# A batched 64x64 matmul kernel: four of the eight a tiles are loaded two product tiles later

## The chip, the cores and the metric

The kernel runs on one core of a Trainium2 chip. The metric is the device time of one execution in microseconds (us), as the median of several runs. One more execution was recorded by the hardware profiler. All rows of "the profile" and "the trace" come from that one.

## The reference

```python
def setup_inputs():
    return {
        "a": np.random.randn(1024, 64, 64).astype(np.float32),
        "b": np.random.randn(1024, 64, 64).astype(np.float32),
    }

def reference(a, b):
    return np.matmul(a, b).astype(np.float32)
```

There are 1024 independent products of two 64x64 matrices. The inputs and the output are fp32 and take 16.8 MB each.

## The kernel before

**Tiles.** The work is cut into 16 *product tiles*, t = 0 to 15, of 64 products each. Product tile t needs one *b tile* of 1 MB, called b t below, and half of an *a tile*. There are eight a tiles, s = 0 to 7, of 2 MB each. a tile s serves the product tiles 2s and 2s + 1. Each product tile ends in a *store* of 1 MB, called store t.

**Loads.** An a tile comes in four parts (`load_a`). Three of them go through GpSimd's (POOL's) DMA queue and are turned into bf16 on the way (line 74). The fourth stays fp32 and goes through SyncE's (SP's) DMA queue (line 78). The first a tile is loaded in another way and plays no part here. b tiles (`load_b`, line 97) go through SP's queue for even t and through ScalarE's (ACT's) queue for odd t. Stores go through POOL's queue (line 195), and only the last two product tiles are stored through SP's and ACT's. So POOL's queue carries most of each a tile and most stores, one after the other, and SP's queue carries the fourth parts of the a tiles and half of the b tiles.

**Work on a product tile.** TensorE needs a transposed. For s = 2 to 5 VectorE (DVE) does it, with 32x32 block transposes (line 128, `transpose_dve`), one half of the a tile per product tile, after ACT has cast the fp32 part (line 126). For the other a tiles DVE first copies the tile into one bf16 tile (`regroup`, lines 109 and 112), TensorE transposes (line 138) and ACT copies the result out of PSUM (line 141). Then DVE copies the blocks of one product tile into a block-diagonal operand (`spread`, lines 154 and 164) and casts the b tile to bf16 (`cast`, line 173; the last one is shared with ACT, lines 178 and 180). TensorE multiplies (line 218), ACT copies the product to SBUF (line 206), and the store is issued one product tile later.

**Buffers.** There are three buffers for a tiles 1 to 7 and three for b tiles, eight for output tiles. a tile 4 goes where a tile 1 was, a tile 5 where a tile 2 was, and so on. Loading b tile t + 3 has to wait for the cast of b tile t.

**Order.** The order of the instructions is written out by hand (`tc.manual_schedule()`). Each engine executes its own instructions in that order, and a DMA is issued by the engine that owns its queue, in that engine's order. In the pass of the loop for product tile t the order is: spread and cast of tile t + 1, load of b tile t + 3, now and then a load of an a tile, the multiplication of tile t, preparation of the a tile that is two further on, and the store of tile t - 1. Before the loop, a tiles 0, 1 and 2 and b tiles 0, 1 and 2 are asked for. a tiles 3 and 4 are asked for in the pass t = 0, then a tiles 5, 6 and 7 in the passes t = 2, 4 and 6.

The preparation of a tile s on DVE starts in the pass t = 2s - 4 (from s = 3 on). So a tile 6 is regrouped in the pass t = 8, after the cast of b tile 9, and a tile 7 in the pass t = 10, after the cast of b tile 11. Both are on DVE, which runs in order: what comes later in its order (the spread and cast for tile 12 behind a tile 7) waits with it.

Of the kernel before, what the change touches and what calls it, by code (L numbers as in the profile page):

```python
# [13 lines left out]
def kernel(  # L14
# [19 lines left out]
    n_t, n_s = B // 64, B // 128  # L34
    A_AHEAD = 3
# [34 lines left out]
    def load_a(s):  # L70

        a_sb = a_pool.tile([128, 3, 16, 64], bf16, name="a_sb")
        for h in range(3):
            nc.gpsimd.dma_start(  # L74
                out=a_sb[:, h, :, :].rearrange("p v k -> p (v k)"), in_=a_v[s, h], single_packet=True
            )
        a_raw = a_pool.tile([128, 16, 64], fp32, name="a_raw")
        nc.sync.dma_start(out=a_raw[:].rearrange("p v k -> p (v k)"), in_=a_v[s, 3])
        a_tiles[s] = a_sb, a_raw

    def load_first_a():

        raw = [
            o_pool.tile([128, 8, 2, 2, 64], fp32, name="o_sb")[:].rearrange(
                "p gh j wl n -> p (gh j wl n)"
            )
            for _ in range(2)
        ]
        parts = [raw[h % 2][:, 1024 * (h // 2) : 1024 * (h // 2) + 1024] for h in range(4)]
        for h in range(4):  # L90
            (nc.scalar if h % 2 else nc.sync).dma_start(out=parts[h], in_=a_v[0, h])
        a_tiles[0] = parts

    def load_b(t):
        b_sb = b_pool.tile([128, 16, 128], fp32, name="b_sb")
        queue = nc.scalar if t % 2 else nc.sync
        queue.dma_start(out=b_sb[:], in_=b_v[t])  # L97
        b_tiles[t] = b_sb

    def regroup(s):  # L100
        a_sb = a_tiles.pop(s)
        a_bf = work.tile([128, 16, 4, 64], bf16, name="a_bf")
        if s == 0:
            for h in range(4):
                copy = nc.scalar.copy if h % 2 else nc.vector.tensor_copy
                copy(a_bf[:, :, h, :], a_sb[h].rearrange("p (v k) -> p v k", v=16))  # L106
        else:
            cast_sb, raw = a_sb
            nc.vector.tensor_copy(  # L109
                a_bf[:, :, 0:3, :], cast_sb[:].rearrange("p h v k -> p v h k")  # L110
            )
            nc.vector.tensor_copy(a_bf[:, :, 3, :], raw[:])  # L112
        abf_tiles[s] = a_bf
        at_tiles[s] = work.tile([128, 32, 4, 4, 4], fp32, name="at_sb")

    def transpose_dve(s, half):
        cast_sb, raw = a_tiles[s]
        if half == 0:
            at_tiles[s] = work.tile([128, 4, 8, 4, 4, 4], fp32, name="at_sb")
        for h in (2 * half, 2 * half + 1):  # L120
            rows = cast_sb[:, h, :, :] if h < 3 else None
            if h == 3:
                rows = work.tile([128, 16, 4, 64], bf16, name="a_bf")[:, 0:4, :, :].rearrange(
                    "p x y k -> p (x y) k"
                )
                nc.scalar.copy(rows, raw[:])  # L126
            pairs = rows.rearrange("p v k -> p (v k)").bitcast(fp32)
            nc.vector.transpose(  # L128
                at_tiles[s][:, h].rearrange("p g w mp vo -> p w vo g mp"),
                pairs.rearrange("p (vo w kp) -> p w vo kp", vo=4, w=4),  # L130
            )

    def transpose(s, j):
        a_cols = abf_tiles[s][:].rearrange("p v h k -> p v (h k)").bitcast(fp32)
        for wl in range(2):
            at_ps = t_psum.tile([128, 4, 128], fp32, name="at_ps")
            for vo in range(4):
                nc.tensor.transpose(  # L138
                    at_ps[:, vo, :], a_cols[:, 4 * vo + 2 * j + wl, :], identity[:]
                )  # L140
            nc.scalar.copy(  # L141
                at_tiles[s][:, :, 2 * j + wl, :, :],
                at_ps[:].rearrange("p vo (g mp) -> p g mp vo", mp=4),
            )

    def spread(t):
        bd = bd_tiles[t % N_BD]
        at_sb = at_tiles[t // 2]
        for h in range(4):
            rows = slice(32 * h, 32 * h + 32)  # L150
            if t // 2 in ON_DVE:
                for i in range(2):
                    block = 32 * (2 * (t % 2) + i)
                    nc.vector.tensor_copy(  # L154
                        bd[rows, 8 * i : 8 * i + 8, :, h, :, :].rearrange(
                            "p g w mp vo -> p (g w) (mp vo)"
                        ),
                        at_sb[block : block + 32, h].rearrange(
                            "p g w mp vo -> p (g w) (mp vo)"
                        ),  # L160
                    )
            else:
                half = slice(16 * (t % 2), 16 * (t % 2) + 16)
                nc.vector.tensor_copy(  # L164
                    bd[rows, :, :, h, :, :].rearrange("p g w mp vo -> p (g w) (mp vo)"),
                    at_sb[rows, half].rearrange("p g w mp vo -> p (g w) (mp vo)"),
                )

    def cast(t):
        b_bf = work.tile([128, 16, 128], bf16, name="b_bf")  # L170
        b_sb = b_tiles.pop(t)
        if t < n_t - 1:
            (nc.vector.tensor_copy if t else nc.scalar.copy)(b_bf[:], b_sb[:])  # L173
        else:
            for gq in range(4):
                rows = slice(4 * gq, 4 * gq + 4)
                if gq % 2:
                    nc.vector.tensor_copy(b_bf[:, rows, :], b_sb[:, rows, :])
                else:
                    nc.scalar.copy(b_bf[:, rows, :], b_sb[:, rows, :])  # L180
        bbf_tiles[t] = b_bf

    def store(t):
        for piece in held.pop(t):
            piece()
# [53 lines left out]
    with tc.manual_schedule():  # L239
        load_first_a()  # L240

        nc.vector.memset(warm[:, 0:1], 0.0)
        nc.scalar.copy(warm[:, 1:2], warm[:, 0:1])
        load_b(0)
        load_b(1)
        nc.vector.memset(bd_tiles[0][:], 0.0)  # L246
        make_identity(nc, identity)
        nc.gpsimd.memset(bd_tiles[1][:, 0:8], 0.0)
        load_a(1)
        load_b(2)  # L250
        nc.gpsimd.memset(bd_tiles[1][:, 8:16], 0.0)
        load_a(2)
        regroup(0)
        transpose(0, 0)
        transpose(0, 1)
        spread(0)
        cast(0)
        for t in range(n_t):
            s, half = t // 2, t % 2
            if t + 1 < n_t:  # L260
                spread(t + 1)
                cast(t + 1)
            if t + B_AHEAD < n_t:
                load_b(t + B_AHEAD)
            if half == 0 and 0 < s < n_s - 1 - A_AHEAD:
                load_a(s + 1 + A_AHEAD)
            if half == 0 and 0 < s < n_s - 1 and s + 1 not in ON_DVE:
                transpose(s + 1, 1)
            multiply(t)
            if t == 0:  # L270
                regroup(1)
                load_a(A_AHEAD)
                load_a(A_AHEAD + 1)
                transpose(1, 0)
                transpose(1, 1)
            if t and s + 2 in ON_DVE and (half or s):
                for part in [0, 1] if t == 1 else [half]:
                    transpose_dve(s + 2, part)
                if half:
                    a_tiles.pop(s + 2)  # L280
            elif half == 0 and 0 < s and s + 2 < n_s:
                regroup(s + 2)
            elif half == 1 and s + 2 < n_s:
                transpose(s + 2, 0)
            if t >= HOLD - 1:
                store(t - HOLD + 1)
        for t in range(n_t - HOLD + 1, n_t):
            store(t)
# [30 lines left out]
```

## Time and profile before

| | us |
|---|---|
| median of three runs (lowest, highest) | 134.39 (134.0, 134.44) |
| the profiled execution's own time | 134.24 |
| span of the profiled execution | 132.1 |
| DVE busy | 100.7 (76%) |
| ACT busy | 89.2 (68%) |
| TensorE: matmuls, weight loads | 63.2 (48%), 60.5 (46%) |
| POOL busy | 32.0 (24%) |

How to read it: the span is what the trace covers, and the execution's own time is 2.1 us longer than that. Busy time is an average over the whole span. HBM read 33.55 MB and written 16.78 MB over the span are 381 GB/s. In the rows on DMA, q0 is POOL's queue, q1 is SP's and q10 is ACT's. A DMA row gives the time from the issue of a transfer to the landing of its last byte, which includes everything that stands ahead of it in its queue.

### The profile page before, as it was taken

How to read it: one execution, taken by the hardware profiler on the slowest of the kernel's cores; microseconds unless marked ns; L12 is line 12 of the kernel's file. 1: busy time of each engine (PE TensorE's matmuls, PEld its weight loads, DVE VectorE, ACT ScalarE, POOL GpSimd, SP SyncE). 2: the span in 40 equal slices, each digit the busy share in tenths (PEclk: the TensorE clock that was granted, in tenths of full speed). 3: DMA queues.
4: the chain of work that ended last, by engine and by line, in shares of the span. 5: the costliest groups of instructions: out<-in, count | busy, mean ns of one | idle time of the engine just before them, and what ended most of it. 6: DMA issues, size and time to landing. Idle time of an engine off the chain costs nothing.

```text
span 132.1 us, 2719 instructions
## 1 busy us (share of the span) xinstructions
PE 63.2 (48%) x1088; PEld 60.5 (46%) x1088; DVE 100.7 (76%) x150; ACT 89.2 (68%) x159; POOL 32.0 (24%) x43
## 2 busy tenths in 40 slices
PE   0006406990733701909190737359709834677700
PEld 0006306980733701909190737259709734676700
DVE  5930399209999915999989998999999998598730
ACT  2225524999893790583989197929999996728970
POOL 8991000420074000702061302040203040312000
PEclk9999999999686555555555555555995995555555
DMA  3999999999999999999999999999999999999996
GB/s 83 351 336 310 309 313 277 288 301 327 326 305 385 371 308 298 395 385 396 327 282 357 402 395 347 296 326 387 399 392 394 394 392 387 398 399 396 364 324 201
DMA packets 19020, 44.99 MB, mean 341 GB/s; under 512 B 1088, under 2 KB 3136, under 8 KB 19008
## 3 DMA queue, kind: packets, MB, share of 16 engines
q0 software_dynamic: 6832, 20.19, 50.6%
q1 hardware_dynamic: 7120, 14.68, 30.8%
q10 hardware_dynamic: 5056, 9.96, 20.0%
q8 instruction: 8, 0.13, 0.4%
q14 instruction: 4, 0.03, 0.1%
HBM read 33.55 MB, written 16.78 MB: 381 GB/s over the span
## 4 chain that ended last, share of the span: by engine, by line
DMA 37%; DVE 27%; ACT 13%; PE 9%; issue 8%; ACTq 2%; SPq 1%
DMA b_sb<-in_b_dram 31%; DVE at_bd L154 11%; ACT o_sb L206 11%; DMA o_sb<-in_a_dram 6%; DVE b_bf L173 6%; PE o_ps L218 5%; DVE at_bd L164 4%; PE at_ps L138 3%; DVE at_sb L128 3%; DVE a_bf L109 1%; DVE a_bf L112 1%; ACTq L97 1%; ACT a_bf L126 1%; ACT a_bf L106 1%; ACT at_sb L141 1%
## 5 line engine op out<-in xcount | busy, mean ns | idle before, releaser
L206 ACT COPY o_sb<-o_ps 64x512 f32<-64x512 f32 x116 | 67.4, 581 | 19.2 <-PE o_ps L218 16.1
L218 PEld LDWEIGHTS <-at_bd 128*128 128x128 bf16 x1024 | 50.5, 125 | 52.9 <-DVE b_bf L173 44.7
L218 PE MATMUL o_ps<-b_bf,at_bd 128*128 128x64 bf16 x960 | 49.1, 231 | 49.4 <-DVE b_bf L173 42.7
L164 DVE COPY at_bd<-at_sb 32x1024 f32<-32x1024 f32 x32 | 23.2, 724 | 12.7 <-ACT at_sb L141 11.9
L154 DVE COPY at_bd<-at_sb 32x512 f32<-32x512 f32 x64 | 27.9, 436 | 1.3
L195 POOL DMA_DIRECT2D out_dram<-o_sb x14 | 15.5, 1108 | 47.5 <-ACT o_sb L206 30.7
L74 POOL DMA_DIRECT2D a_sb<-in_a_dram x21 | 12.4, 606 | 39.8 <-DVE at_sb L128 26.4
L173 DVE CAST b_bf<-b_sb 128x2048 bf16<-128x2048 f32 x14 | 17.2, 1227 | 6.4 <-DMA b_sb<-in_b_dram 6.0
L138 PE MATMUL at_ps<-identity,a_bf 128*128 128x128 f32 x64 | 11.2, 349 | 11.2 <-ACT a_bf L106 11.2
L138 PEld LDWEIGHTS at_ps<-identity,a_bf 128*128 128x128 f32 x64 | 10.3, 188 | 11.1 <-issue 11.1
L128 DVE STREAM_TRANSPOSE at_sb<-a_sb 128x512 f32<-128x512 f32 x12 | 12.0, 1062 | 0.0
L141 ACT COPY at_sb<-at_ps 128x512 f32<-128x512 f32 x16 | 8.5, 594 | 2.1 <-PE at_ps L138 2.0
L106 ACT CAST a_bf<-o_sb 128x1024 bf16<-128x1024 f32 x2 | 2.1, 1044 | 5.2 <-DMA o_sb<-in_a_dram 5.2
L128 DVE STREAM_TRANSPOSE at_sb<-a_bf 128x512 f32<-128x512 f32 x4 | 4.2, 1053 | 0.7 <-ACT a_bf L126 0.7
L126 ACT CAST a_bf<-a_raw 128x1024 bf16<-128x1024 f32 x4 | 4.2, 1046 | 0.7 <-DMA a_raw<-in_a_dram 0.6
L173 ACT CAST b_bf<-b_sb 128x2048 bf16<-128x2048 f32 x1 | 1.9, 1898 | 3.7 <-DMA b_sb<-in_b_dram 3.7
L206 DVE COPY o_sb<-at_ps 64x256 f32<-64x256 f32 x8 | 3.4, 422 | 1.3 <-PE at_ps L218 1.2
L246 DVE MEMSET at_bd<- 128x4096 f32 x1 | 3.5, 3472 | 0.8 <-issue 0.8
L218 PE MATMUL at_ps<-b_bf,at_bd 128*128 128x64 bf16 x64 | 3.6, 242 | 1.0 <-DVE at_bd L164 1.0
L106 DVE CAST a_bf<-o_sb 128x1024 bf16<-128x1024 f32 x2 | 2.8, 1385 | 1.7 <-DMA o_sb<-in_a_dram 1.7
L206 ACT COPY o_sb<-at_ps 64x256 f32<-64x256 f32 x8 | 2.9, 367 | 0.1
L180 ACT CAST b_bf<-b_sb 128x512 bf16<-128x512 f32 x2 | 1.1, 616 | 2.8 <-DMA b_sb<-in_b_dram 2.8
(16 smaller groups left out, 15.4 us busy)
## 6 DMA issues: line engine op xcount, KB each, us to landing
out_dram<-o_sb POOLq DMA_DIRECT2D x14, 1024.0 KB, 21.1
a_sb<-in_a_dram POOLq DMA_DIRECT2D x21, 256.0 KB, 16.0
a_raw<-in_a_dram SPq DMA_DIRECT2D x7, 512.0 KB, 16.9
o_sb<-in_a_dram SPq DMA_DIRECT2D x2, 512.0 KB, 5.8
o_sb<-in_a_dram ACTq DMA_DIRECT2D x2, 512.0 KB, 7.1
out_dram<-o_sb SPq DMA_DIRECT2D x2, 512.0 KB, 3.6
out_dram<-o_sb SPq DMA_DIRECT2D x2, 256.0 KB, 3.6
out_dram<-o_sb ACTq DMA_DIRECT2D x2, 256.0 KB, 3.1
```

Source lines behind the costliest of these rows:

```text
L74: nc.gpsimd.dma_start(out=a_sb[:, h, :, :].rearrange("p v k -> p (v k)"), in_=a_v[s, h], single_packet=True)
L106: copy(a_bf[:, :, h, :], a_sb[h].rearrange("p (v k) -> p v k", v=16))
L126: nc.scalar.copy(rows, raw[:])
L128: nc.vector.transpose(at_tiles[s][:, h].rearrange("p g w mp vo -> p w vo g mp"), pairs.rearrange("p (vo w kp) -> p w vo kp", vo=4, w=4),)
L138: nc.tensor.transpose(at_ps[:, vo, :], a_cols[:, 4 * vo + 2 * j + wl, :], identity[:])
L141: nc.scalar.copy(at_tiles[s][:, :, 2 * j + wl, :, :], at_ps[:].rearrange("p vo (g mp) -> p g mp vo", mp=4),)
L154: nc.vector.tensor_copy(bd[rows, 8 * i : 8 * i + 8, :, h, :, :].rearrange("p g w mp vo -> p (g w) (mp vo)"), at_sb[block : block + 32, h]. ...
L164: nc.vector.tensor_copy(bd[rows, :, :, h, :, :].rearrange("p g w mp vo -> p (g w) (mp vo)"), at_sb[rows, half].rearrange("p g w mp vo -> p ...
L173: (nc.vector.tensor_copy if t else nc.scalar.copy)(b_bf[:], b_sb[:])
L195: store_queue(t, lo).dma_start(out=o_v[t, :, lo : lo + n, :], in_=o_sb[:, lo : lo + n].rearrange("p gh j wl n -> p (gh j wl n)"),)
L206: copies[2 * par + wl](dst, src)
L218: nc.tensor.matmul(o_ps[:, gl, g % 2, j, :], at_bd[:, j, g, :, u], b_bf[:, g, 64 * u : 64 * u + 64], start=(u == 0), stop=(u == 1),)
```

## The change

a tile 4 is asked for in the pass t = 2 and no longer at the end of the pass t = 0. a tiles 5, 6 and 7 are asked for in the passes t = 4, 6 and 8 and no longer in t = 2, 4 and 6. No instruction is added or removed, and the buffers stay as they are.

```diff
-            if half == 0 and 0 < s < n_s - 1 - A_AHEAD:
-                load_a(s + 1 + A_AHEAD)
+            if half == 0 and 0 < s < n_s - A_AHEAD:
+                load_a(s + A_AHEAD)
             if half == 0 and 0 < s < n_s - 1 and s + 1 not in ON_DVE:
                 transpose(s + 1, 1)
             multiply(t)
             if t == 0:
                 regroup(1)
                 load_a(A_AHEAD)
-                load_a(A_AHEAD + 1)
                 transpose(1, 0)
                 transpose(1, 1)
```

The order that this gives in the two queues concerned, as compiled (a4 is the part of a tile 4 that goes through that queue, s0 is store 0):

```
POOL before:  a1 a2 a3 a4 s0 a5 s1 s2 a6 s3 s4 a7 s5 s6 s7 ... s13
POOL after:   a1 a2 a3 s0 a4 s1 s2 a5 s3 s4 a6 s5 s6 a7 s7 ... s13
SP before:    a0 b0 a1 b2 a2 a3 a4 b4 a5 b6 a6 b8 a7 b10 b12 b14
SP after:     a0 b0 a1 b2 a2 a3 b4 a4 b6 a5 b8 a6 b10 a7 b12 b14
```

## The prediction

> **What bounds the kernel now.** I read the page's slices first (forty slices of 3.3 us).
>
> ```profile
> DMA  3999999999999999999999999999999999999996
> GB/s 83 351 336 310 309 313 277 288 301 327 326 305 385 371 308 298 395 385 396 327 282 357 402 395 347 296 326 387 399 392 394 394 392 387 398 399 396 364 324 201
> ```
>
> The 16 DMA engines are busy from the second slice to the last but one. (GB/s dips while a tiles come in, because it counts the bf16 bytes written, half of those read.) The change moves no byte, so it can only gain where DMA stands idle. Stretches of one us at the end show how much that is (the last two columns are DMA share and GB/s):
>
> ```profile
> 122.00:123.00 1.00, 1.00 (x23) 1.00 (x21) 0.00 (x0) 0.96 (x3) 0.00 (x0) 0.50 1.02 393
> 123.00:124.00 1.00, 1.00 (x23) 1.00 (x21) 0.91 (x3) 0.99 (x2) 0.00 (x0) 0.50 0.96 370
> 125.00:126.00 1.00, 0.00 (x0) 0.00 (x0) 0.97 (x3) 0.95 (x4) 0.00 (x0) 0.50 0.74 262
> 126.00:127.00 1.00, 0.00 (x0) 0.00 (x0) 0.54 (x2) 0.96 (x3) 0.00 (x0) 0.50 0.98 335
> 127.00:128.00 1.00, 0.00 (x0) 0.00 (x0) 0.00 (x0) 0.96 (x4) 0.00 (x0) 0.50 1.04 341
> ```
>
> Against the usual 1.03 the shares 0.96, 0.74 and 0.98 miss 0.07 + 0.29 + 0.05 = 0.41 us. That is nearly all there is to win: the last product tiles could be stored a little sooner. A loss has no such limit.
>
> Next the waits, for what orders the work in between:
>
> ```profile
> POOL a_sb L74 <- DVE at_sb L128: 26.4, 3, 11.4
> POOL a_sb L74 <- DVE a_bf L109: 11.7, 1, 11.7
> DVE b_bf L173 <- DMA b_sb<-in_b_dram: 6.0, 3, 4.2
> ```
>
> POOL stands before each a load until DVE has freed a buffer, 38 us in all. DVE waits for b tiles three times only: 4.24 us before the cast of b 4, later 0.41 (b 13) and 1.37 (b 14). Between 51.2 and 109 it is never idle for more than 0.4 us, so DVE paces that stretch while DMA works off a backlog of stores. The timeline has the places that the change touches:
>
> ```profile
> 51.18 1.23 DVE L173 CAST b_bf<-b_sb 128x2048 bf16<-128x2048 f32 x1 [4.24 <-DMA b_sb<-in_b_dram]
> 87.27 0.96 DVE L109 COPY a_bf<-a_sb 128x3072 bf16<-128x3072 bf16 x1
> 98.94 0.95 DVE L109 COPY a_bf<-a_sb 128x3072 bf16<-128x3072 bf16 x1
> 103.53 1.23 DVE L173 CAST b_bf<-b_sb 128x2048 bf16<-128x2048 f32 x1
> 104.84 14.37 DMA b_sb<-in_b_dram
> ```
>
> They are the cast of b 4, the regroup of a 6, that of a 7, the cast of b 12, and (from the chain) b 15: issued when b 12 is cast and landed at 119.2, from where the chain runs to the end, over ACT's casts and copies.
>
> **Part 1, b 4 (a gain).** On SP the load of b 4 stood behind the fourth part of a 4, which waited for the regroup of a 1 (ends 23.85). b 4 was issued at 24.87 and took 26.3 us. Now it needs only the cast of b 1, which ends at 22.4. The larger gain is in the queue: a 4's 0.52 MB no longer stand ahead of it. SP's queue moved 0.65 MB between 36.4 and 40.2, when it took a 4's part, so 0.52 MB are 3.1 us; with some of the earlier issue I take 3.5 us. The bounds are 0, if SP's earlier entries drain late, and 4.24, the whole wait. From the cast of b 4 on DVE then runs 3.5 us early, for as long as nothing else is late.
>
> **Part 2, what is late next.** Queues are served in order. In POOL's queue a 6 is now the last of the set a 1 to a 6 and stores 0 to 4. Before, the same set ended with store 4. So the new landing of each a tile can be read from the old landing of a store: a 4 from store 0, a 5 from store 2, a 6 from store 4, a 7 from store 6. The DMA view of the moments at which stores 0, 2, 4 and 6 were issued (28.03, 41.12, 59.42, 72.96) gives us to landing:
>
> ```profile
> out_dram<-o_sb POOLq DMA_DIRECT2D x1, 1024.0 KB, 19.6
> out_dram<-o_sb POOLq DMA_DIRECT2D x1, 1024.0 KB, 24.5
> out_dram<-o_sb POOLq DMA_DIRECT2D x1, 1024.0 KB, 24.1
> out_dram<-o_sb POOLq DMA_DIRECT2D x1, 1024.0 KB, 25.8
> ```
>
> Landings: 47.6, 65.6, 83.5 and 98.8. DVE wants the tiles, 3.5 us earlier than before, at 56.0 (a 4, first transposes 59.46), 70.0 (a 5, 73.51), 83.8 (a 6) and 95.4 (a 7). a 4 and a 5 have slacks of 8.4 and 4.4 us, a 6 one of 0.3, and a 7 is 3.4 us late. So the lead is gone at a 7 and the regroup of a 7 stays near 98.9.
>
> It may come later still. With b loads 3.5 us ahead, SP's and ACT's queues have moved more by then. A product tile takes (103.53 - 51.18) / 8 = 6.5 us, so the lead is 3.5 / 6.5 x 1.05 = 0.56 MB, or 1.4 us at 0.40 MB per us, that POOL's queue lacks. Bounds: 0 and 1.4, or 4 us if a 6 is late too and its wait comes on top. I take 1.4, because DMA is full throughout: a 7 lands at 100.2, the regroup is 1.3 us later than before, and so is the cast of b 12 behind it on DVE (104.8).
>
> **Part 3, the end.** b 15 is issued 1.3 us later, at 106.1, by ACT, which has its copies behind that. It took 14.4 us. It will share less: b 14 hangs on the cast of b 11, ahead of the regroup in DVE's order, so it keeps its 3.5 us and leaves earlier. With three queues active (109.5 to 114) q10 moved 0.48 MB in 4.5 us, 0.107 per us; with two (116 to 117) 0.137. 3.5 us at the higher rate are 0.105 MB, 0.8 us. b 15 lands at 106.1 + 14.4 - 0.8 = 119.7, 0.5 us later. DVE's own chain takes the 1.3 us without harm: b 13 and b 14 have landed, and their waits of 0.41 and 1.37 us go. Everything from b 15's landing on keeps its length.
>
> **Edits at no cost.** The 21 issues on POOL (0.57 us each) are the same, moved; POOL is 24% busy, so even all 12 of the moved ones in the open, 6.8 us, lie in its idle time. a 4 to a 7 no longer wait for a buffer there, but their queue is served in order behind the stores, so the 38 us are worth nothing by themselves. Stores 0, 1, 3 and 5 move ahead of an a tile; nobody waits for them (output tiles have eight buffers). On SP the fourth parts follow b 4, 6, 8 and 10; b 10 landed at 73.7 + 14.6 = 88.3, so a 7's fourth part is there some 4 us later, before the 99.8 at which it is read.
>
> **The sum.** +1.3 - 0.8 = +0.5 us. The profiled execution, 134.24, lies 0.15 under the median; on the median it is 134.39 + 0.5 = 134.9.
>
> **Two rules against the rows.** First: a 7 landed at 90.5 (issued at 68.4, 22.1 us) and was read at 98.9, and these 8.4 us of cover are given up here. The Trainium skill, "DMA: Bandwidth & Descriptors", Rules for kernel authors, says to issue a DMA early and wait for it late. By the rule alone, without b 4's gain, the wait for a 7 would show whole, 3.4 + 1.4 us, and the time would be near 139. Second: with two queues active q0 moved 0.26 MB and q10 0.14 in the same us, and b 4 took 26.3 us where b 15 took 14.4. The same page (Issuing engines are not separate DMA queues) says that all queues interleave on the same 16 engines and that spreading issues saves issue time only. Read strictly, the order changes nothing (134.4); the rows say that the place in a queue decides when a tile is there.
>
> **Rivals.**
>
> *A tile 7 is in time, and the end fills up (faster).* If POOL's queue gets through its set by about 97.5, a part of the lead reaches b 15. For it: a load needs no write to HBM at its end, the store that I read it from does. Against it: the full DMA rows. DMA limits the gain to 0.41 us, or 0.7 if the packets mix a little better: 133.7 to 134.0.
>
> *Nothing moves (the same).* b 15 lands within 0.4 us of before, because DMA is full and what b loads gain a tiles lose: 134.0 to 134.8. It needs a 7 at 98.8 to 100.
>
> *a 6 is late as well (much slower).* Its slack is 0.3 us. If its wait eats the lead and a 7 still comes at 102 or later, the cast of b 12 is 3 us late, DVE's 1.78 us of old waits no longer cover it, and the end goes out by 1.5 to 2.2: 135.9 to 136.6.
>
> **How the numbers follow.** 0.3%, about 0.4 us, is what a measurement of this kernel can tell from no change. Forecast (slower by 0.4 to 1.4) 0.40; a 7 in time 0.23; nothing moves 0.28; a 6 late too 0.09. So faster 0.23, same 0.28, slower 0.49. The range runs from 133.7 (the DMA limit) to 136.4 (most of the last case); the forecast's own is 134.8 to 135.8.
>
> **What would show it.** Right: no wait over 1 us before the cast of b 4; a wait of 3 to 6 us of DVE's line 109 for a_sb, which the profile before does not have; the cast of b 12 at 104 to 106; b 14 landed by 112; POOL's waits on DVE for a buffer gone. Wrong: line 109 never waits (then a 7 was served sooner than the order of the queue says), the wait falls on a 6 or a 5 (lines 109 or 128 earlier), or DMA shares under 0.95 before 119.

## The result, and the profile after

The changed kernel takes 135.05 us, the median of 17 runs (134.51 to 135.81). The kernel before takes 134.33 in the runs beside it. The ratio is 1.0056, with a 95% interval of 1.0043 to 1.0068: slower by 0.7 us. The profiled execution took 135.27 us with a span of 133.2, which is 1.03 and 1.1 us more than before.

The profile's slices show that DMA is still full until the last few slices, and that these are now less full than before:

```profile
DMA  2999999999999999999999999999999999999885
GB/s 69 370 335 311 305 312 280 285 305 380 399 320 305 344 403 397 361 324 306 372 385 407 350 276 335 408 394 361 287 313 392 397 405 388 400 400 362 302 274 199
```

The waits answer to those shown of before (who waits, for whom, us in total, times, the longest):

```profile
DVE a_bf L109 <- DMA a_sb<-in_a_dram: 6.5, 2, 5.2
DVE b_bf L173 <- DMA b_sb<-in_b_dram: 0.8, 1, 0.8
POOL a_sb L74 <- DMA out_dram<-o_sb: 6.5, 3, 5.4
```

The first wait is new: DVE stands before the regroup until an a tile has landed. The second was 6.0 us and is 0.8. POOL's waits for DVE to free a buffer, 38 us before, are gone. In their place POOL waits 6.5 us for stores to finish, which the last section takes up.

The timeline at the same places:

```profile
47.67 1.23 DVE L173 CAST b_bf<-b_sb 128x2048 bf16<-128x2048 f32 x1 [0.83 <-DMA b_sb<-in_b_dram]
84.40 0.96 DVE L109 COPY a_bf<-a_sb 128x3072 bf16<-128x3072 bf16 x1 [1.25 <-DMA a_sb<-in_a_dram]
94.56 1.23 DVE L173 CAST b_bf<-b_sb 128x2048 bf16<-128x2048 f32 x1
101.02 0.96 DVE L109 COPY a_bf<-a_sb 128x3072 bf16<-128x3072 bf16 x1 [5.23 <-DMA a_sb<-in_a_dram]
105.36 1.23 DVE L173 CAST b_bf<-b_sb 128x2048 bf16<-128x2048 f32 x1
```

These are the casts of b 4 and b 11, the regroups of a 6 and a 7, and the cast of b 12. The cast of b 4 comes 3.51 us earlier than before (51.18). The cast of b 11 is still 3.24 us early (97.80 before). Then DVE waits 5.23 us for a 7, the wait that the change adds. After that the regroup is 2.08 us late and the cast of b 12 is 1.83 us late. The chain that ended last tells the rest:

```profile
77.31 23.59 DMA a_sb<-in_a_dram
106.67 13.55 DMA b_sb<-in_b_dram
```

a 7's third part lands at 100.9. b 15 is issued at 106.67 (before: 104.84) and lands at 120.2 (119.2). From there on the kernel is what it was, 1 us later: from b 15's landing to the end of the span it takes 12.9 us in both kernels. The DMA shares at the end (second last column) show what that means:

```profile
124.00:125.00 1.00, 0.00 (x0) 0.00 (x0) 0.95 (x3) 0.99 (x2) 0.00 (x0) 1.00 0.62 225
126.00:127.00 1.00, 0.00 (x0) 0.00 (x0) 0.43 (x1) 0.95 (x4) 0.00 (x0) 1.00 0.34 115
127.00:128.00 1.00, 0.00 (x0) 0.00 (x0) 0.00 (x0) 0.96 (x3) 0.00 (x0) 0.53 0.85 290
```

Before, one such stretch fell to 0.74. Now three fall to 0.62, 0.34 and 0.85, because the last stores are issued about 1 us later, too late to keep DMA busy. The lost time shows as idle DMA at the end, though its cause lies at 95 to 101.

### The profile page after: what moved, and what is told of

Same layout as the page of the kernel before. It is cut to its first block, busy times and chain, and to the rows that moved or that the text cites. A ratio compares the mean times of both kernels' runs of the same rounds, so it can differ in the third digit from the quotient of the medians.

```text
span 133.2 us, 2719 instructions
## 1 busy us (share of the span) xinstructions
PE 59.7 (45%) x1088; PEld 56.8 (43%) x1088; DVE 99.5 (75%) x150; ACT 89.5 (67%) x159; POOL 30.8 (23%) x43
## 4 chain that ended last, share of the span: by engine, by line
DMA 51%; issue 28%; POOL 7%; ACT 6%; DVE 4%; POOLq 0%; DVEq 0%; ACTq 0%
DMA a_sb<-in_a_dram 25%; DMA out_dram<-o_sb 16%; DMA b_sb<-in_b_dram 10%; ACT o_sb L206 5%; POOL a_sb L74 3%; POOL out_dram L195 3%; DVE at_bd L164 2%; POOL at_bd L248 1%; DVE b_bf L173 1%; ACT b_bf L180 1%; DVE a_bf L112 1%; POOL identity masks.py:199 0%; POOL identity masks.py:197 0%; DVE a_bf L109 0%; POOLq L195 0%
## 5 line engine op out<-in xcount | busy, mean ns | idle before, releaser
L218 PEld LDWEIGHTS <-at_bd 128*128 128x128 bf16 x1024 | 47.4, 120 | 52.0 <-DVE b_bf L173 42.7
L218 PE MATMUL o_ps<-b_bf,at_bd 128*128 128x64 bf16 x960 | 47.6, 227 | 48.1 <-DVE b_bf L173 40.6
L195 POOL DMA_DIRECT2D out_dram<-o_sb x14 | 14.1, 1010 | 81.0 <-ACT o_sb L206 60.6
L154 DVE COPY at_bd<-at_sb 32x512 f32<-32x512 f32 x64 | 27.3, 427 | 1.4
L138 PE MATMUL at_ps<-identity,a_bf 128*128 128x128 f32 x64 | 10.6, 336 | 14.8 <-ACT a_bf L106 11.2
L138 PEld LDWEIGHTS at_ps<-identity,a_bf 128*128 128x128 f32 x64 | 9.6, 178 | 14.9 <-issue 11.2
L109 DVE COPY a_bf<-a_sb 128x3072 bf16<-128x3072 bf16 x3 | 2.9, 958 | 6.5 <-DMA a_sb<-in_a_dram 6.5
L206 DVE COPY o_sb<-o_ps 64x512 f32<-64x512 f32 x4 | 2.8, 690 | 0.5 <-ACT o_sb L206 0.5
```

The lines of the kernel that those rows point to most:

```text
L138: nc.tensor.transpose(at_ps[:, vo, :], a_cols[:, 4 * vo + 2 * j + wl, :], identity[:])
L154: nc.vector.tensor_copy(bd[rows, 8 * i : 8 * i + 8, :, h, :, :].rearrange("p g w mp vo -> p (g w) (mp vo)"), at_sb[block : block + 32, h]. ...
L195: store_queue(t, lo).dma_start(out=o_v[t, :, lo : lo + n, :], in_=o_sb[:, lo : lo + n].rearrange("p gh j wl n -> p (gh j wl n)"),)
L206: copies[2 * par + wl](dst, src)
L218: nc.tensor.matmul(o_ps[:, gl, g % 2, j, :], at_bd[:, j, g, :, u], b_bf[:, g, 64 * u : 64 * u + 64], start=(u == 0), stop=(u == 1),)
```

## The experiments

The theory, called Q, is the prediction's: what counts is a 7's place in POOL's queue, behind stores 5 and 6. It makes DVE wait, and it eats the lead that b 4 gives. Rival M: the new order of stores and loads costs DMA itself, whichever a tile is late. Rival C: each a tile asked for later costs some cover. Rival L, for two of the runs: the lead of b 4 is worth something to the end. The kernel before ran beside each kernel, with medians of 134.36 to 134.42; each ratio is to those runs (it is not exactly the quotient of the medians given, but the quotient always lies within its interval). Diffs are against the changed kernel unless they say otherwise.

**1. a tile 7 back at its old place.**

```diff
-            if half == 0 and 0 < s < n_s - A_AHEAD:
+            if half == 0 and 0 < s < n_s - 1 - A_AHEAD:
                 load_a(s + A_AHEAD)
+            if t == 6:
+                load_a(7)
```

> a tile 7 asked for at its old place (pass t = 6), a tiles 4, 5 and 6 late as in the changed kernel. Theory Q (a tile 7's place in POOL's queue behind stores 5 and 6 is the whole loss): a tile 7 lands at 91 to 94, no wait for it on DVE, the cast of b 12 at 100 to 102, b 15 lands before 119; DMA limits the gain, so 133.8 to 134.2, at or under before (134.33). Rival M (the new order of stores and loads costs DMA itself, whichever a tile is late): nearly all of the loss stays, 134.8 to 135.1. Rival C (every a tile that is asked for later costs some cover): about a quarter of the loss goes, 134.8.

134.06 us, ratio 0.9969 (0.9951 to 0.9988): faster than before. The whole loss goes, and more. a 6 is still waited for, by 1.65 us, but the regroup of a 7 waits for nothing, and the cast of b 12 comes 4.1 us earlier than in the changed kernel:

```profile
85.35 0.96 DVE L109 COPY a_bf<-a_sb 128x3072 bf16<-128x3072 bf16 x1 [1.65 <-DMA a_sb<-in_a_dram]
96.65 0.96 DVE L109 COPY a_bf<-a_sb 128x3072 bf16<-128x3072 bf16 x1
101.28 1.23 DVE L173 CAST b_bf<-b_sb 128x2048 bf16<-128x2048 f32 x1
```

M and C fall. a tiles 4, 5 and 6 may come late at no cost in time: the wait for a 6 takes a part of the lead, but the cast of b 12 is still 2.25 us earlier than before the change. The loss is a 7's alone.

**2. a tile 7 behind one store, and behind three.** Like experiment 1, with `if t == 7:` and with `if t == 9:` (in the second, a 7's fourth part also stands behind b 12 on SP).

> As the changed kernel, but a tile 7 asked for one product tile earlier (pass t = 7), so that it stands behind store 5 and no longer behind store 6. A store of 1 MB takes POOL's queue about 5 us there. Q: a tile 7 lands at 95.5 to 97 instead of 100.9, the wait for it falls from 5.2 us to under 1.5, the cast of b 12 at 101 to 102.5, 133.9 to 134.3. M (the order costs DMA itself): half of the loss stays, 134.6 to 134.8.

> As the changed kernel, but a tile 7 asked for one product tile later still (pass t = 9), behind stores 5, 6 and 7. Q: it lands at about 106, the wait for it on DVE is about 10 us, the cast of b 12 moves from 105.4 to about 110, and as the old waits for b 13 and b 14 have nothing left to give, the end moves by nearly the whole 5 us less what b 15 gains from emptier queues: 137 to 139.5. M: another 0.3 to 0.5 us, 135.4 to 135.6.

One store: 134.00 us, ratio 0.9978 (0.9967 to 0.9989). Three stores: 139.41 us (four runs), ratio 1.0398 (1.0371 to 1.0426). The regroup of a 7, first behind one store and then behind three (there with the cast of b 12):

```profile
96.97 0.96 DVE L109 COPY a_bf<-a_sb 128x3072 bf16<-128x3072 bf16 x1 [0.93 <-DMA a_sb<-in_a_dram]
```

```profile
105.95 0.96 DVE L109 COPY a_bf<-a_sb 128x3072 bf16<-128x3072 bf16 x1 [9.60 <-DMA a_sb<-in_a_dram]
110.29 1.23 DVE L173 CAST b_bf<-b_sb 128x2048 bf16<-128x2048 f32 x1
```

With the changed kernel and experiment 1 this makes a row:

| stores from store 5 on ahead of a 7 | wait for a 7 | cast of b 12 at | time |
|---|---|---|---|
| none | 0 | 101.28 | 134.06 |
| 1 | 0.93 | 101.69 | 134.00 |
| 2 (the change) | 5.23 | 105.36 | 135.05 |
| 3 | 9.60 | 110.29 | 139.41 |
| (before: none, without the lead) | 0 | 103.53 | 134.3 to 134.4 |

Up to a cast of b 12 at about 102 the time does not move. From two stores to three the wait grows by 4.37 us and the time by 4.36. So the wait is free until it has eaten the slack, and what comes on top costs about its length. With three stores the end no longer hangs on b 15, which lands at 118.4, earlier than in any row but the first two: the chain that ended last runs from a 7's landing mostly over DVE's own work.

**3. Only a tile 7 late.** Against the kernel before:

```diff
-            if half == 0 and 0 < s < n_s - 1 - A_AHEAD:
+            if half == 0 and 0 < s < n_s - 2 - A_AHEAD:
                 load_a(s + 1 + A_AHEAD)
+            if t == 8:
+                load_a(7)
```

> Only a tile 7 late (behind stores 5 and 6), the others at their old places, so without the lead from b 4. Q: the 4.2 us wait before the cast of b 4 is back; a tile 7 lands where store 6 landed, at 98.8 to 99.5, and is read at about 98.9: a wait under 0.6 us, 134.2 to 134.6. It would show that a tile 7 costs only in so far as it is later than it was read before. M and C: half of the loss or more, 134.7 to 135.0.

134.71 us, ratio 1.0021 (1.0000 to 1.0042), 0.1 us over what Q allowed and at the lower end of the rivals' range, so the time alone decides nothing. The trace is close to Q: the wait before the cast of b 4 is back at 4.08 us, and a 7 is waited for by 0.72 us (Q allowed 0.6) and regrouped 0.5 us later than before:

```profile
99.42 0.96 DVE L109 COPY a_bf<-a_sb 128x3072 bf16<-128x3072 bf16 x1 [0.72 <-DMA a_sb<-in_a_dram]
```

**4. b 4's gain taken away.** As the changed kernel, with the fourth part of a 4 at its old place on SP, ahead of b 4. The load is split into `load_a_cast` (three parts on POOL) and `load_a_raw` (one on SP); the lines that split it are left out here:

```diff
             if half == 0 and 0 < s < n_s - A_AHEAD:
-                load_a(s + A_AHEAD)
+                load_a_cast(s + A_AHEAD)
+                if s == 1:
+                    a_tiles[4] = a_cast[4], raw4
+                else:
+                    load_a_raw(s + A_AHEAD)
...
                 load_a(A_AHEAD)
+                raw4 = a_pool.tile([128, 16, 64], fp32, name="a_raw")
+                nc.sync.dma_start(
+                    out=raw4[:].rearrange("p v k -> p (v k)"), in_=a_v[4, 3]
+                )
```

> As the changed kernel, but the fourth part of a tile 4 at its old place on SP, ahead of b 4: the gain of part 1 is undone. Q as the prediction summed it: the 4 us wait before the cast of b 4 is back, DVE and the b loads run 3 us later, POOL's queue gets more of the DMA engines before a tile 7, which lands at 99 to 99.8 and is read within 1 us of where it was read before the change; b 15 is issued at 105 to 105.5 and takes 14.4 us; 134.5 to 134.9, not slower than the changed kernel although a gain is taken away. Rival L (the lead of b 4 is worth something to the end): slower than the changed kernel, 135.3 or more.

134.61 us, ratio 1.0013 (0.9994 to 1.0032), faster than the changed kernel (1.0043 to 1.0068) although it loses 3.7 us at the cast of b 4. The splitting of the function shifts line numbers by 7, so lines 173 and 109 are 180 and 116 here:

```profile
51.38 1.23 DVE L180 CAST b_bf<-b_sb 128x2048 bf16<-128x2048 f32 x1 [4.52 <-DMA b_sb<-in_b_dram]
99.82 0.96 DVE L116 COPY a_bf<-a_sb 128x3072 bf16<-128x3072 bf16 x1 [1.55 <-DMA a_sb<-in_a_dram]
```

a 7 is regrouped at 99.82 instead of 101.02. So the lead from b 4 does make a 7 land 1.2 us later; the prediction put 1.4 on it. The bytes show how: by 98.7 us the queues of SP and ACT have moved 19.90 MB in the changed kernel and 19.44 here, POOL's queue 12.86 MB there and 13.25 here. L falls: when a wait for a 7 follows, the lead is worse than nothing.

**5. Only a tile 4 late.** Against the kernel before, `load_a(4)` moves to the pass t = 2.

> Only a tile 4 late, a tiles 5, 6 and 7 at their old places. Q: the wait before the cast of b 4 falls from 4.2 us to under 1; b 6 still stands behind the same bytes on SP and lands near 63, so DVE waits up to 2 us there and keeps a lead of 1.5 to 2; a tiles 6 and 7 are in time; 133.9 to 134.3. M: between, 134.4 to 134.6. C: 134.4 to 134.6.

134.13 us, ratio 0.9968 (0.9952 to 0.9984), as Q said. The wait before the cast of b 4 is gone, b 6 is waited for by 2.14 us, the cast of b 12 is at 101.29, and b 15 lands at 102.60 + 14.93 = 117.5.

**6. The change split by queues.** The fourth parts late and the cast parts at their old places, and the reverse. The lines that split `load_a` are left out again.

```diff
 (fourth parts late, against the kernel before)
             if half == 0 and 0 < s < n_s - 1 - A_AHEAD:
-                load_a(s + 1 + A_AHEAD)
+                load_a_cast(s + 1 + A_AHEAD)
+            if half == 0 and 0 < s < n_s - A_AHEAD:
+                load_a_raw(s + A_AHEAD)
...
-                load_a(A_AHEAD + 1)
+                load_a_cast(A_AHEAD + 1)
```

> The fourth parts of a tiles 4 to 7 (SP's queue) late as in the changed kernel, the three cast parts (POOL's queue) at their old places. Q: b 4 lands near 47, DVE leads by about 3.5 us, no wait for a tile 6 or 7; b 15 lands at 116 to 118; the end is limited by DMA, 133.6 to 134.0, faster than before. M: POOL's order is that of before, so 134.2 to 134.4. C: 134.4 to 134.6.

> The other half of the split by queues: the cast parts of a tiles 4 to 7 (POOL) late as in the changed kernel, the fourth parts (SP) at their old places, so that b 4, 6, 8 and 10 stand behind them as before. Q: no lead from b 4, a tile 7 lands at 98.8 to 100 behind stores 5 and 6, a wait of up to 1.6 us, 134.4 to 134.8, under the changed kernel's 135.05. L: without the lead it is slower than the changed kernel, 135.3 or more.

Cast parts late: 134.62 us, ratio 1.0011 (0.9995 to 1.0026), a wait for a 7 of 1.73 us (Q allowed 1.6). It agrees with experiment 4: without the lead a 7 lands at 99.5 here and at 99.7 there.

```profile
99.62 0.96 DVE L116 COPY a_bf<-a_sb 128x3072 bf16<-128x3072 bf16 x1 [1.73 <-DMA a_sb<-in_a_dram]
```

Fourth parts late: 134.59 us, ratio 1.0000 (0.9982 to 1.0017), a miss. Up to b 15 it goes as Q said: no wait for an a tile, and b 15 lands at 101.50 + 14.56 = 116.1, 3.1 us before the old 119.2. But the end does not move. DMA has nothing to spare: the stretches from 120 to 129 stand at a share of 1.00 or more, and then there is a tail:

```profile
128.00:129.00 1.00, 0.00 (x0) 0.00 (x0) 0.00 (x0) 0.00 (x0) 0.00 (x0) 0.50 1.07 369
129.00:130.00 1.00, 0.00 (x0) 0.00 (x0) 0.00 (x0) 0.00 (x0) 0.00 (x0) 0.50 0.70 247
130.00:131.00 1.00, 0.00 (x0) 0.00 (x0) 0.00 (x0) 0.00 (x0) 0.00 (x0) 0.50 0.19 65
```

The dips of before are filled, as the prediction's limit supposed, but a part of the 16 engines is busy almost as long as before (share 0.19 after 130). In experiments 1, 2 (one store) and 5, where b 15 lands at 116.9 to 117.5, a similar tail leaves a gain of 0.3 to 0.4 us.

Where the rest goes can be read from the semaphores in the traces. At the end SyncE waits for the DMAs' semaphores one after another, in a fixed order. The wait for SP's last store comes first and that for ACT's last store is the last, and a wait that is already met takes 0.06 us. In experiment 1 (profiled execution 134.16 us) ACT's store lands last, at 131.13, when SyncE has only that wait left, and the span ends 0.92 us later. With the fourth parts late (134.62 us) SP's store lands last, at 131.16. Then seven more waits follow, and the span ends 1.34 us later. That is 0.42 of the 0.46 us between the two spans. In neither does the last landing come much earlier than before the change (131.21). This compares one execution of each kernel, and no run changes the order of these waits alone.

**7. Is the end bound by DMA's work?** Store 14 goes from SP's queue, where it moves in packets of 1 KB, to POOL's, where stores move in packets of 4 KB.

```diff
 (the first against experiment 5, which stores tile 14 in halves)
-        if t < n_t - 2:
+        if t < n_t - 1:
             return nc.gpsimd
...
-            whole = t < n_t - 2
+            whole = t < n_t - 1
```

The other three keep `whole` as it was, so store 14 stays in halves: on experiment 5, on experiment 1, and on the fourth parts late of experiment 6.

> Only a tile 4 late, and store 14 moved from SP's queue (1 KB packets) to POOL's (4 KB packets). With a tile 4 late alone b 15 landed near 117.5 and the last stores took 4.4 to 5.0 us to land instead of 3.1 to 3.6, so the end looked bound by DMA and no longer by ACT's chain. If DMA work is the bound, 1 MB at 42 ns per KB and engine instead of 48 saves 0.4 us: 133.5 to 133.9. If the chain through ACT is the bound, nothing: 134.0 to 134.3.

> Only a tile 4 late, and store 14 on POOL's queue as two stores of half a tile, as it is on SP's queue otherwise. With the whole tile in one store the DMA share fell to 0.91, 0.82 and 0.73 in the three us from 123, because that store was issued only when the whole tile was copied (124.35). If that gap ate the saving, halves close it: 133.6 to 133.9. If POOL's queue is no better for store 14 at all: 134.1 to 134.4.

> a tile 7 at its old place, a tiles 4, 5 and 6 late, and store 14 on POOL's queue in halves. Q with DMA as the bound at the end: 133.5 to 133.9, the fastest so far. If the end is bound by ACT's chain or by the queue that finishes last: 134.0 to 134.3, as without the move.

> The fourth parts late, the cast parts at their old places (which gave b 15 at 116.1 and no gain), with store 14 on POOL's queue in halves. There the last stores of SP's queue took 7.3 us to land, the longest of all, behind 1 MB of store 14 in 1 KB packets. If that queue, finishing last, ate the gain: 133.9 to 134.2. If not: 134.4 to 134.7 as before the move, and what ate the gain stays open.

| store 14 on POOL | time | ratio | without the move |
|---|---|---|---|
| experiment 5, whole | 134.35 | 1.0004 (0.9989 to 1.0019) | 134.13 |
| experiment 5, halves | 134.12 | 0.9976 (0.9961 to 0.9991) | 134.13 |
| experiment 1, halves | 134.08 | 0.9969 (0.9957 to 0.9981) | 134.06 |
| fourth parts late, halves | 134.30 | 0.9988 (0.9974 to 1.0002) | 134.59 |

As one whole store (first row) it was issued only at 124.35, when the whole tile was copied, and DMA ran dry meanwhile:

```profile
123.00:124.00 1.00, 0.00 (x0) 0.00 (x0) 0.97 (x3) 0.99 (x2) 0.00 (x0) 1.00 0.91 358
124.00:125.00 1.00, 0.00 (x0) 0.00 (x0) 0.59 (x2) 0.95 (x4) 0.65 (x1) 1.00 0.82 300
125.00:126.00 1.00, 0.00 (x0) 0.00 (x0) 0.00 (x0) 0.95 (x4) 0.23 (x1) 0.57 0.73 231
```

In halves that gap closes, but the expected 0.4 us does not come. So larger packets for store 14 do not bring the end forward. The last row moved by 0.3 us and lies between the two answers expected of it. Its trace fits what experiment 6 shows: SP's queue no longer lands last, and the span ends 1.05 us after the last landing and no longer 1.34. Of the 0.41 us by which the span is shorter, 0.29 lie there and 0.11 at the last landing. Five kernels that lose the wait for a 7, or all but 0.93 us of it, and keep some lead end at 134.0 to 134.1 (experiments 1, 2 with one store, 5, and 7 in halves on 1 and 5); those that end later are the two with the fourth parts late and the one with the whole store. Experiments 1 and 5 beat both kernels: by 0.3% the one before, by 0.9 to 1.0 us the changed one.

## Why the prediction was right, point by point

**The forecast.** Slower, 134.9 (134.8 to 135.8); measured 135.05. The rise of the median, 0.72 us, was forecast at 0.5.

**b 4 (part 1).** 3.5 us were taken and 3.51 measured. It was issued at 23.39, 1 us later than I had it (22.4), and took 24.3 us. The place in the queue gave the most, as assumed: on SP's queue the fourth part of a 3 landed at 38.2 before and at 37.9 after, and before the change a 4's part, landing at 40.8, stood between it and b 4.

**Landings from old stores (part 2).** a 4 and a 5 were put at 47.6 and 65.6 and landed at 47.4 and 65.9. a 6 was put at 83.5 from store 4, 0.3 us before its need. It landed at 84.3, and DVE, 4.2 us early by then and not 3.5, wanted it at 83.15 and waited 1.25 us. So a 6 was late, as one of the rivals had it. That should hardly have mattered to the time, because DVE had to wait for a 7 anyway. a 7 was put at 98.8 from store 6, plus 1.4 for the b loads ahead: 100.2. It landed at 100.9, 0.7 later. Experiments 4 and 6 (cast parts late) separate the two terms. Without the lead a 7 landed at 99.7 and 99.5, so the lead cost 1.2 to 1.4 us, as summed, and the reading from store 6 was 0.7 to 0.9 us too early. Why a 7 lands that much after store 6's old place is open.

**The end (part 3).** b 15 was to be issued at 106.1 and land at 119.7 after 13.6 us. It was issued at 106.67, took 13.55 and landed at 120.2. b 14 left early as assumed: issued at 95.88, it landed 13.8 us later at 109.7 (115.2 before).

**The mis-sized term** in the sum is a 7's landing, in its first part, the reading from store 6: +0.7 us at the landing and 0.8 at the regroup, of which 0.5 reached b 15. The profiled execution, 1.03 us longer, has just that on top of the 0.5.

**The signs.** Those named for "right" all came: b 4 waited for by 0.83 us, 5.23 us before a 7's regroup, b 12 cast at 105.36, b 14 landed at 109.7, POOL's waits for a buffer gone. One named for "wrong" came in part: a wait of 1.25 us fell on a 6. The other two did not: line 109 did wait, and DMA shares were 1.00 or more in every us from 20 to 119.

**Edits at no cost.** No cost of theirs shows, with one thing missed: POOL gained a wait. a 7's third part was issued at 77.31, only once store 4 had landed at 77.03; both count on the same semaphore. a 7's three parts landed at 96.7, 98.7 and 100.9, so the third was 2.2 us behind the second. In experiment 3, where POOL issued the third without such a wait, it was 2.4 us behind. So the queue ahead of them, not the issue, set when they landed.

**The rules.** The prediction put 139 on the rule to issue early (the Trainium skill, "DMA: Bandwidth & Descriptors", Rules for kernel authors). That sum was wrong. The 3.4 us in it count from a need that b 4's gain had moved 3.5 us forward, and the case was meant to be without that gain. Without it, experiments 3, 4 and 6 (cast parts late) measured waits for a 7 of 0.72 to 1.73 us and 134.6 to 134.7 us. So the lead covered nothing of a 7's lateness; it made DVE ready earlier and a 7 later. Of the four loads issued later, three cost no time (experiment 1). By the same page's statement that all queues interleave on the same 16 engines (Issuing engines are not separate DMA queues), read as no effect of order, it would have been 134.4; 135.05 and experiment 2's 139.41 speak against that reading.

**The rivals.** "a 7 in time" is what experiments 1 and 2 built, and its price, 133.7 to 134.0, was right but for 0.1 us. "a 6 is late as well" had its first condition (1.25 us), but a 7 came at 100.9 and not at 102 or later. The DMA limit of 0.41 us held: by the medians no kernel gained more than 0.36 us, by the ratios none more than 0.43, within their intervals.

## What to carry to other kernels

Where DMA is full, a load that is asked for later is not a local matter: find what it now stands behind in its queue, and read its new landing from the last transfer of the same set in the old order. Then follow the first tile whose slack is gone, along the in-order engine that waits for it, to the loads that this engine releases. A lead won early is worth only what the next wait leaves of it, and it can make that wait longer, because the transfers that run ahead take bandwidth from the one that is late.

## What the runs showed of the hardware

**A transfer's time is mostly what shares DMA with it.** b 15, always 1 MB, took 13.5 to 14.9 us in these kernels, and 6.8 us in the kernel with a 7 behind three stores. There it was issued at 111.60, after b 14 had landed, and 1.2 MB of other transfers moved while it was under way; in the changed kernel it was 4.3 MB. (The view gives 0.5 KB as the size of b loads; the queue's bytes, 1.05 MB in that stretch, show the 1 MB.)

```profile
b_sb<-in_b_dram ACTq DMA_DIRECT2D x1, 0.5 KB, 6.8
```

**An issue can wait for an older transfer.** On POOL's queue, DMAs waited for others several places ahead of them to land, though they share no data. a 7's third part waited 5.38 us for store 4, eight DMAs ahead of it, which counts on the same semaphore:

```profile
77.31 0.53 POOL L74 DMA_DIRECT2D a_sb<-in_a_dram  x1 [5.38 <-DMA out_dram<-o_sb]
```

**The mean share hides that the engines do not end together.** With the dips at the end filled, the share of the 16 DMA engines fell to 0.7 and then to 0.1 or 0.2 over the last 2 us, so work gained on the average did not all become time. In the kernel with the fourth parts late 11 packets were in flight at 129.25, 9 at 130.0 and 2 at 130.5; before the change there were still 16 at 130.5.

**The order of the last landings can count.** SyncE's waits at the end took 0.06 us each. When the store that is waited for first landed last, the span ended 1.34 us after that landing, otherwise 0.9 to 1.1 us (experiments 6 and 7).
